# Half of the seven-product FFN's passes with the same weights joined to 512 columns, on one Trainium2 core

## The chip, the cores and the metric

The kernel runs on one core of one Trainium2 chip. Its engines each work through their own queue in order: TensorE (PE) multiplies, VectorE (DVE) and ScalarE (ACT) do the elementwise work, GpSimd (POOL) mainly issues accumulating DMAs, SyncE (SP) issues loads. The metric is the device time of one execution in microseconds.

## The reference

Two decoder layers on 512 tokens of width 1024, in fp32, and a final norm. Each layer has a token mixer, a cross-attention (both with the residual added) and then the gated MLP, on which most of this case turns:

```python
def conv_ffn(x, norm, w_up, dw_w, dw_b, w_down):
    h = rms_norm(x, norm) @ w_up
    g = causal_dwconv(h[..., :D_FF], dw_w, dw_b)
    u = h[..., D_FF:]
    return (jax.nn.gelu(g) * u) @ w_down
```

`D_FF` is 3072, the convolution is 3 tokens wide. The cross-attention's query is `rms_norm(x, norm) @ wq`.

## The kernel before, in words

Activations lie transposed, 128 channels by 512 tokens in a tile (T = 512, M = T/2 = 256, C = 8 tiles of x). An fp32 operand is split into a high part (`high`, a rounding copy by ACT) and a low part (`low`, a subtraction by DVE); a product is three matmuls, high x high, high x low and low x high (`mm3`, lines 186 to 188). A norm keeps its factor r apart: `Norm.feed` multiplies a tile of x by the gain and splits it, the mean of the squares is got by a product with ones into a PSUM bank of its own (`stat`, one buffer; lines 287 and 288), and r is multiplied in later.

The MLP's up-projection makes 24 chunks of 128 gate and 128 value channels. Chunks 0 and 1 are plain products (`start` in `opening`, 24 matmuls of 512 columns each). Each chunk from 2 (`first`) on is a `unit`: a 2 x 2 block product (gate and value by left and right half of the tokens) by seven products in place of eight. A product is four blocks of three matmuls of 256 columns. Chain G adds a11 x B11 and a12 x B21 and gives the gate's left half. Chain F starts as a copy of the first of these (ACT, line 928), then adds s2 x T2, s3 x T3 and a22 x T4; it is read three times, after s2 (into `u`, left), after s3 (into `u`, right) and at the end (the value's left half). Chain H adds s1 x T1 and s4 x B22; with `u` it gives both right halves. The B operands are halves of the norm's tiles, the T operands sums of halves made ahead.

The weights a11, a12, a22, z and r are loaded; s1 to s4 come from them by accumulating DMAs on POOL (lines 825, 828, 830), each issued behind a `low`, and are then split (ACT line 815, DVE line 822). One PSUM pool (`main_ps`) serves G, F and H. The order in a unit, on every engine, is that of the code in `unit`: TensorE has s1, s2, a12, s3, then from unit 4 on the down-projection of an earlier group of four chunks (24 matmuls of 512 columns, tile `aux`), then a11 of the next unit (`ahead`), s4 and a22. `gating` of a unit is a generator whose pieces run in the next unit (`next(left)`): add of H, multiplication by r, the convolution's first tap on ACT (line 895), the other two on DVE (line 898), gelu, the product with f (line 914), and the split of the result (lines 917 and 919), which the down-projections use. The down weights' split is lines 200 (ACT) and 203 (DVE).

At an MLP's opening the plain products cover the mean and r. The tiles of x get their last contribution just before, so the order of `start`'s blocks is made such that the last tile and the mean come late.

## Time and profile before

| | |
|---|---|
| median of three runs | 1432.15 us (1432.05 to 1433.4) |
| profiled execution | 1431.55 us |
| its span | 1429.8 us |
| mean granted TensorE clock | 0.999 |
| TensorE busy | 1417.3 us, 99% of the span |
| VectorE, ScalarE busy | 1074.0 and 900.6 us |

A row of a timeline has the start in us, the duration, engine and line, the operation with what it writes and reads, and in brackets the idle time of its engine ahead of it with what ended that. TensorE's matmuls overlap: one of 256 columns lasts 0.28 us, and the next begins 0.12 us after it. DVE and ACT instructions overlap by about 0.1 us.

### The profile page before, as it was taken

The numbers are of one execution on the slowest core, as the hardware profiler recorded it, in microseconds if no ns is written. First come the engines' busy times: TensorE is split into PE (matmuls) and PEld (weight loads), VectorE is DVE, ScalarE is ACT, GpSimd is POOL, SyncE is SP. The second block draws the span as 40 slices with busy tenths as digits, with TensorE's granted clock in tenths as the row PEclk, the third lists the DMA queues.
The fourth block names the chain that finished last, engine by engine and source line by source line (L and its number), as shares of the span: only waits on it lengthen the run. The fifth ranks groups of instructions, "written<-read, shape, count | busy, mean of one in ns | idle before, by whom it ended". The sixth has DMA issues, their size and how long they took to land.

```text
span 1429.8 us, 22834 instructions
## 1 busy us (share of the span) xinstructions
PE 1417.3 (99%) x8650; PEld 1261.6 (88%) x8650; DVE 1074.0 (75%) x1796; ACT 900.6 (63%) x1592; POOL 316.9 (22%) x333
## 2 busy tenths in 40 slices
PE   9999999999999999999999999999999999999998
PEld 7888888998999999999988777899889999999997
DVE  6987776778776676667798997978787676676665
ACT  7678754667555666666665547667665665666664
POOL 0011310210122222222008992010002222222111
PEclk9999999999999999999999999999999999999999
DMA  8522232544487777777432354345438777777741
GB/s 303 195 75 103 89 124 76 119 110 147 99 199 165 171 172 166 168 171 167 133 133 89 119 162 148 108 87 139 118 86 197 175 177 164 170 175 164 175 120 60
DMA packets 80031, 204.33 MB, mean 143 GB/s; under 512 B 9008, under 2 KB 9520, under 8 KB 79920
## 3 DMA queue, kind: packets, MB, share of 16 engines
q1 hardware_dynamic: 50832, 150.15, 32.8%
q0 software_dynamic: 28800, 52.44, 21.5%
q8 instruction: 68, 1.11, 0.3%
q14 instruction: 43, 0.35, 0.1%
q10 hardware_dynamic: 288, 0.27, 0.1%
HBM read 145.16 MB, written 2.10 MB: 103 GB/s over the span
## 4 chain that ended last, share of the span: by engine, by line
PE 89%; DVE 4%; POOL 2%; ACT 2%; issue 1%; DMA 1%; SPq 0%; POOLq 0%; DVEq 0%; ACTq 0%
PE mm L188 21%; PE mm L186 21%; PE mm L187 21%; PE aux L187 7%; PE aux L186 7%; PE aux L188 7%; PE mm L458 2%; DVE wlo L167 1%; DMA raw<-in_wv 1%; POOL actf L1498 1%; ACT whi L166 1%; PE aux L532 0%; POOL act L167 0%; POOL tmp L1319 0%; DMA raw<-in_wo 0%
## 5 line engine op out<-in xcount | busy, mean ns | idle before, releaser
L186 PE MATMUL mm<-act,whi 128*128 128x512 f32 (+2 forms) x1061 | 368.9, 349 | 0.7 <-ACT act L274 0.6
L187 PE MATMUL mm<-act,whi 128*128 128x512 f32 (+2 forms) x1061 | 369.1, 348 | 0.3 <-DVE act L181 0.2
L188 PE MATMUL mm<-act,wlo 128*128 128x512 f32 (+2 forms) x1061 | 369.0, 348 | 0.0
L186 PEld LDWEIGHTS mm<-act,whi 128*128 128x128 f32 x1061 | 200.5, 189 | 28.3 <-ACT act L274 1.3
L187 PEld LDWEIGHTS mm<-act,whi 128*128 128x128 f32 x1061 | 200.7, 189 | 27.4 <-DVE act L167 1.0
L188 PEld LDWEIGHTS mm<-act,wlo 128*128 128x128 f32 x1061 | 200.7, 189 | 25.1 <-DVE wlo L167 0.6
L822 DVE TENSOR_TENSOR bigr<-raw,bigr 128x512 fp32r<-128x512 f32 x176 | 120.8, 688 | 131.6 <-ACT bigr L815 127.9
L188 PE MATMUL mm<-bigr,bigr 128*128 128x256 f32 x704 | 199.4, 283 | 1.7 <-DVE bigr L822 1.7
L186 PE MATMUL mm<-bigr,bigr 128*128 128x256 f32 x704 | 199.2, 283 | 0.0
L187 PE MATMUL mm<-bigr,bigr 128*128 128x256 f32 x704 | 199.2, 283 | 0.0
L815 ACT ACTIVATE bigr<-raw 128x512 fp32r<-128x512 f32 x176 | 109.0, 621 | 79.1 <-DVE wlo L203 75.9
L828 POOL DMA_DIRECT2D raw<-wa x100 | 87.9, 899 | 309.0 <-DVE bigr L822 215.2
L186 PE MATMUL aux<-act,whi 128*128 128x512 f32 x399 | 155.7, 390 | 0.0
L187 PE MATMUL aux<-act,whi 128*128 128x512 f32 x399 | 155.7, 390 | 0.0
L188 PE MATMUL aux<-act,wlo 128*128 128x512 f32 x399 | 155.2, 389 | 0.0
L166 ACT ACTIVATE whi<-raw 128x1024 fp32r<-128x1024 f32 (+1 forms) x95 | 96.5, 1020 | 87.6 <-PE mm L187 45.2
L188 PEld LDWEIGHTS mm<-bigr,bigr 128*128 128x128 f32 x704 | 135.1, 192 | 2.1 <-DVE bigr L822 2.1
L186 PEld LDWEIGHTS mm<-bigr,bigr 128*128 128x128 f32 x704 | 135.2, 192 | 0.0
L187 PEld LDWEIGHTS mm<-bigr,bigr 128*128 128x128 f32 x704 | 135.2, 192 | 0.0
L825 POOL DMA_DIRECT2D raw<-raw x50 | 43.2, 864 | 366.5 <-DVE wlo L822 347.3
L167 DVE TENSOR_TENSOR wlo<-raw,whi 128x1024 fp32r<-128x1024 f32 (+1 forms) x75 | 90.3, 1210 | 19.5 <-ACT whi L166 19.0
L188 PEld LDWEIGHTS aux<-act,wlo 128*128 128x128 f32 x399 | 74.9, 188 | 15.8
(353 smaller groups left out, 3040.8 us busy)
## 6 DMA issues: line engine op xcount, KB each, us to landing
raw<-wa POOLq DMA_DIRECT2D x150, 256.0 KB, 3.4
wa<-in_wpair SPq DMA_DIRECT2D x88, 256.0 KB, 3.7
raw<-in_wpair SPq DMA_DIRECT2D x44, 512.0 KB, 3.8
big<-in_wdown SPq DMA_DIRECT2D x42, 512.0 KB, 4.4
raw<-raw POOLq DMA_DIRECT2D x50, 256.0 KB, 3.7
raw<-in_pw SPq DMA_DIRECT2D x24, 512.0 KB, 3.3
raw<-in_win SPq DMA_DIRECT2D x20, 512.0 KB, 3.3
raw<-in_wk SPq DMA_DIRECT2D x16, 512.0 KB, 3.3
```

Source lines behind the costliest of these rows:

```text
L166: A.activation(hi, src, AF.Copy)
L167: fetched[1] = (eng or V).tensor_tensor(lo, src, hi.bitcast(F32), op=ALU.subtract)
L186: PE.matmul(ps, wh, xh, start=first, stop=False, skip_group_check=onto)
L187: PE.matmul(ps, wh, xl, start=False, stop=False, skip_group_check=onto)
L188: return PE.matmul(ps, wl, xh, start=False, stop=last, skip_group_check=onto)
L458: PE.matmul(p, m[j], x, start=k == 0 and j == 0 and x is hi, stop=k == C - 1 and x is lo)
L815: A.activation(self.w[name][0], self.block(name), AF.Copy)
L822: V.tensor_tensor(lo, self.block(name), hi.bitcast(F32), op=ALU.subtract)
L825: G.dma_start(self.r, self.z, accum_op=ALU.add)
L828: G.dma_start(block, self.a22, accum_op=ALU.add)
L1498: G.tensor_tensor(z[:, s:], z[:, s:], f[:, s:], op=ALU.add)
```

## The change

The norm's tiles and the T operands are kept as [high | low] of one half of the tokens, 256 + 256 columns, so that the weight's high part meets both in one matmul of 512 columns. For units 4 to 23 (`c > second`) the five products of G and F are, per block, one matmul of 512 columns and one of 256 (the weight's low part by the operand's high). The sum then lies in two halves of a bank, and `gather` adds them when it is read: an ACT copy of the right half and a DVE add of the left. s1 and s4 stay as they were, but H now lies in the `stat` bank. G and F take a full bank each, and F's seed copies 512 columns. For units 4 and 5 one more matmul writes F's bank, ahead of the seed.

r is multiplied into the whole 512 columns of g and of f, from SBUF. Since the norm's tiles lie by halves, `feed` works in two halves, and the plain products (`start`) and the attention's `query` are done in two halves of 256 columns. The opening's order is changed, and in unit 3 the down weights' split is moved behind that of s1 and s2.

```diff
@@ -209 +209 @@
         return hi[:, i : i + n], lo[:, i : i + n]
 
 
+    def parts(x):
+        return x[:, :M], x[:, M:]
+
@@ -218 +221 @@
 
         def feed(self, c):
             g = col(self.gain[0], self.gain[1] + c)
-            hi, lo = act_r(), act_r()
-            A.activation(hi, X[c], AF.Copy, scale=g)
-            self.last = V.scalar_tensor_tensor(lo, X[c], g, hi.bitcast(F32), op0=ALU.mult, op1=ALU.subtract)
-            self.x[c] = (hi, lo)
+            self.x[c] = act_r(), act_r()
+            halves = [(parts(x), X[c][:, i * M : (i + 1) * M]) for i, x in enumerate(self.x[c])]
+            for (hi, _), x in halves:
+                A.activation(hi, x, AF.Copy, scale=g)
+            for (hi, lo), x in halves:
+                self.last = V.scalar_tensor_tensor(lo, x, g, hi.bitcast(F32), op0=ALU.mult, op1=ALU.subtract)
@@ -473 +478 @@
 
         def query(n, w):
             ps = mm_ps()
-            for i, k in enumerate(PAIRED):
-                mm3(ps, blk(w, k * P), norm.x[k], i == 0, i == C - 1)
+            for half in range(2):
+                for i, k in enumerate(PAIRED):
+                    mm3(parts(ps)[half], blk(w, k * P), parts(norm.x[k][half]), i == 0, i == C - 1)
@@ -740 +746 @@
         def fourth(self, k):
-            split(self.t4[:, k * M : (k + 1) * M], *[x[:, M:] for x in self.norm.x[k]])
+            split(self.t4[:, k * M : (k + 1) * M], *parts(self.norm.x[k][1]))
 
@@ -760 +766 @@
             if self.t4 is not None:
                 t4 = self.t4[:, at]
             V.scalar_tensor_tensor(t4, t2, -1.0, b21, op0=ALU.mult, op1=ALU.subtract)
-            for (hi, _), t in zip(self.t, (t1, t2, t3, t4)):
-                A.activation(hi[:, at], t, AF.Copy)
+            both = [self.block(self.T1 + j, k) for j in range(len(self.t))]
+            for x, t in zip(both, (t1, t2, t3, t4)):
+                A.activation(x[:, :M], t, AF.Copy)
             yield
-            for (hi, lo), t in zip(self.t, (t1, t2, t3, t4)):
-                V.tensor_tensor(lo[:, at], t, hi[:, at].bitcast(F32), op=ALU.subtract)
+            for x, t in zip(both, (t1, t2, t3, t4)):
+                V.tensor_tensor(x[:, M:], t, x[:, :M].bitcast(F32), op=ALU.subtract)
+
+        def block(self, j, c):
+
+            if j - self.T1 == len(self.t):
+                return self.norm.x[c][1]
+            if j >= self.T1:
+                return self.t[j - self.T1][c // 2][:, c % 2 * T : (c % 2 + 1) * T]
+            return self.norm.x[c if j == self.B11 else c + 4][j == self.B22]
 
         def product(self, ps, w, j, first=True):
+
             for c in range(4):
-                if j - self.T1 == len(self.t):
-                    x = blk(self.norm.x[c], M, M)
-                elif j >= self.T1:
-                    x = blk(self.t[j - self.T1], c * M, M)
+                (wh, wl), x = blk(w, c * P), self.block(j, c)
+                if ps.shape[-1] == T:
+                    steps = [(ps, wh, x), (ps[:, :M], wl, x[:, :M])]
+                    for i, (to, part, by) in enumerate(steps if c < 3 else steps[::-1]):
+                        PE.matmul(
+                            to, part, by, start=first and c == 0 and i == 0, stop=c == 3 and i == 1, skip_group_check=True
+                        )
                 else:
-                    x = blk(self.norm.x[c if j == self.B11 else c + 4], M if j == self.B22 else 0, M)
-                mm3(ps, blk(w, c * P), x, first and c == 0, c == 3, not first)
+                    mm3(ps, (wh, wl), parts(x), first and c == 0, c == 3, not first)
             return ps
@@ -900 +918 @@
+        def gather(out, ps):
+
+            A.activation(out, ps[:, M:], AF.Copy)
+            add(out, ps[:, :M], out)
+
         def gating(c, g, f, u, F, H):
-            add(g[:, right_half], H, u[:, :M])
-            V.tensor_tensor(g[:, right_half], g[:, right_half], norm.r[:, right_half], op=ALU.mult)
+            if c > second:
+                add(g[:, right_half], H, u[:, :M])
+                V.tensor_tensor(g, g, norm.r, op=ALU.mult)
+            else:
+                add(g[:, right_half], H, u[:, :M])
+                V.tensor_tensor(g[:, right_half], g[:, right_half], norm.r[:, right_half], op=ALU.mult)
             conv = gate_conv(c, g)
             y = next(conv)
             yield
-            times_r(f, F, left_half)
+            if c > second:
+                gather(f[:, left_half], F)
+                V.tensor_tensor(f, f, norm.r, op=ALU.mult)
+            else:
+                times_r(f, F, left_half)
             next(conv)
             yield
             next(conv)
@@ -923 +954 @@
 
         def ahead(c):
 
-            G, F = main_ps()[:, :M], main_ps()[:, :M]
+            G = bank(c)
+            F = bank(c) if c > second else parts(main_ps())[1]
             m(c, G, "a11", seven.B11)
+            if c in (second + 1, second + 2):
+                w = pairs[c].w["a11"]
+                PE.matmul(F, w[0][:, :P], seven.block(seven.B11, 0), start=True, stop=True)
             A.activation(F, G, AF.Copy)
             return G, F
+
+        def bank(c):
+            return main_ps() if c > second else main_ps()[:, :M]
 
         def unit(c):
 
             nonlocal left, chains
             G, F = chains
             down, seeded = downs.get(c), c > GC
-            H = main_ps()[:, :M]
+            H = stat_ps()[:, :M]
             m(c, H, "s1", seven.T1)
             if c <= second:
                 high(c + 1, "s3")
@@ -943 +981 @@
 
             m(c, F, "s2", seven.T2, False)
             u, f, g = tmp_f(), tmp_f(), tmp_f()
-            A.activation(u[:, :M], F, AF.Copy)
+            if c > second:
+                gather(u[:, :M], F)
+            else:
+                A.activation(u[:, :M], F, AF.Copy)
             if c == first:
                 both(c + 2, "a11")
             if down:
@@ -961 +1002 @@
                 high(c + 2, "a11")
             low(c, "s4")
             if c > second:
-                times_r(g, G, left_half)
+                gather(g[:, left_half], G)
 
             m(c, F, "s3", seven.T3, False)
-            A.activation(u[:, M:], F, AF.Copy)
+            if c > second:
+                gather(u[:, M:], F)
+            else:
+                A.activation(u[:, M:], F, AF.Copy)
             add(f[:, right_half], H, u[:, M:])
             if c <= second:
                 times_r(g, G, left_half)
             if c == second:
                 low(c + 2, "a11")
             low(c + 1, "a22")
-            V.tensor_tensor(f[:, right_half], f[:, right_half], norm.r[:, right_half], op=ALU.mult)
+            if c <= second:
+                V.tensor_tensor(f[:, right_half], f[:, right_half], norm.r[:, right_half], op=ALU.mult)
             both(c + 2, "a11")
             high(c + 1, "a12")
             low(c + 1, "a12")
@@ -983 +1028 @@
                 pairs[c + 3].load()
             if c + 2 in pairs and c > first:
                 pairs[c + 2].load_second()
-            if c >= GC - 1 and c + 1 in downs:
+            if c > second and c + 1 in downs:
                 downs[c + 1].w.high()
                 downs[c + 1].w.low()
             if c + 2 in downs and first < c <= CF - 2:
@@ -992 +1037 @@
             low(c + 1, "s1")
             high(c + 1, "s2")
             low(c + 1, "s2")
+            if c == second:
+                downs[c + 1].w.high()
+                downs[c + 1].w.low()
             if down:
                 down.home(0, d[0], seeded)
 
@@ -1010 +1058 @@
             nonlocal left, chains
             ps, y = {}, {}
 
-            def start(i, ks=range(C)):
-                if ks[0] == 0:
+            def start(i, half, ks=range(C)):
+                if half == 0 and ks[0] == 0:
                     ps[i] = main_ps()
                 for k in ks:
-                    mm3(ps[i], blk(w[i], k * P), norm.x[k], k == 0, k == C - 1)
+                    mm3(parts(ps[i])[half], blk(w[i], k * P), parts(norm.x[k][half]), k == 0, k == C - 1)
 
@@ -1036 +1084 @@
             ss = split(norm.ss)
-            start(0, range(C - 1))
-            start(1, range(2))
-            start(0, (C - 1,))
+            start(0, 0, range(C - 1))
+            start(1, 0, range(C - 1))
+            start(0, 0, (C - 1,))
             fetch(2)
             w[-1].low()
             mean = mean_of(ss)
@@ -1048 +1096 @@
...
             V.reciprocal(norm.r, root)
-            start(1, range(2, C))
+            start(1, 0, (C - 1,))
+            start(0, 1)
+            start(1, 1)
@@ -1062 +1112 @@
-            start(2)
+            start(2, 0)
+            start(2, 1)
@@ -1074 +1125 @@
-            start(3)
+            start(3, 0)
+            start(3, 1)
             chains = ahead(first)
```

DVE's queue between units 3 and 4 of layer 0, before (`bigr` are the low parts of the s weights; row 2 is the low of a12, rows 4 and 5 those of s1 and s2, all of unit 4; L203 is the down weights' low; `mm_3892` is H of unit 3):

```order
L974 TENSOR_TENSOR tmp_3926<-tmp_3926,r_3611 128x256
L822 TENSOR_TENSOR wlo_3802<-wa_3651,whi_3801 128x512
L203 TENSOR_TENSOR wlo_3983<-big_3653,whi_3982 128x1024
L822 TENSOR_TENSOR bigr_3988<-raw_3647,bigr_3988 128x512
L822 TENSOR_TENSOR bigr_3991<-raw_3647,bigr_3991 128x512
L171 TENSOR_TENSOR tmp_3927<-mm_3892,tmp_3925 128x256
L905 TENSOR_TENSOR tmp_3927<-tmp_3927,r_3611 128x256
```

The same place in the change (line 840 is the old 822; `stat_4068` is H of unit 3, and the same bank takes s1 of unit 4):

```order
L1019 TENSOR_TENSOR tmp_4102<-tmp_4102,r_3706 128x256
L840 TENSOR_TENSOR wlo_3978<-wa_3779,whi_3977 128x512
L840 TENSOR_TENSOR bigr_4160<-raw_3775,bigr_4160 128x512
L840 TENSOR_TENSOR bigr_4163<-raw_3775,bigr_4163 128x512
L203 TENSOR_TENSOR wlo_4168<-big_3781,whi_4167 128x1024
L171 TENSOR_TENSOR tmp_4103<-stat_4068,tmp_4101 128x256
L932 TENSOR_TENSOR tmp_4103<-tmp_4103,r_3706 128x256
```

The lows of s1 and s2 now stand ahead of the down weights' low, and the add of H stays right behind all three.

DVE's queue where unit 4 gives way to unit 5, in the change (L929 and L938 are r, L916 the two taps, `mm_4172` is F of unit 4, `mm_4332` F of unit 5):

```order
L171 TENSOR_TENSOR tmp_4237<-stat_4211,tmp_4235 128x256
L929 TENSOR_TENSOR tmp_4237<-tmp_4237,r_3706 128x512
L171 TENSOR_TENSOR tmp_4236<-mm_4172,tmp_4236 128x256
L938 TENSOR_TENSOR tmp_4236<-tmp_4236,r_3706 128x512
L916 SCALAR_TENSOR_TENSOR tmp_4366<-tmp_4237,par,tmp_4366 128x511
L916 SCALAR_TENSOR_TENSOR tmp_4366<-tmp_4237,par,tmp_4366 128x510
L171 TENSOR_TENSOR tmp_4394<-mm_4332,tmp_4394 128x256
```

The add on F after s2 (last row) is a DVE row that was not there, as one ACT copy read F at this point; and the value's left half is gathered and multiplied ahead of the taps.

TensorE's queue at the mean of layer 1's opening, in the change (L292 and L293 are the mean; the 27 rows of 512 columns and the three of tile 7 that led to it are now 42 and three of 256):

```order
L186 MATMUL mm_10899<-act_10871,whi_10885 128x256
L187 MATMUL mm_10899<-act_10871,whi_10885 128x256
L188 MATMUL mm_10899<-act_10871,wlo_10886 128x256
L292 MATMUL stat_10952<-act_10895,ones 128x512
L293 MATMUL stat_10952<-act_10896,ones 128x512
L186 MATMUL mm_10921<-act_10871,whi_10889 128x256
```

Tile 7 of the second piece and all of the right halves now stand behind the mean.

## The prediction

> **What bounds the kernel now.** I read the page first (busy time by engine, then the chain that ended last), then the waits of TensorE, then timelines at the places that the change touches.
>
> ```profile
> span 1429.8 us, 22834 instructions
> PE 1417.3 (99%) x8650; PEld 1261.6 (88%) x8650; DVE 1074.0 (75%) x1796; ACT 900.6 (63%) x1592; POOL 316.9 (22%) x333
> PE 89%; DVE 4%; POOL 2%; ACT 2%; issue 1%; DMA 1%; SPq 0%; POOLq 0%; DVEq 0%; ACTq 0%
> ```
>
> TensorE is the bound: 99% busy and 89% of the chain that ended last. So the time moves in two ways only: TensorE's own work gets shorter, or TensorE waits. The waits of TensorE name the two that this change can touch:
>
> ```profile
> PE mm L188 <- DVE bigr L822: 1.7, 2, 0.8
> ...
> PE stat L288 <- DVE act L167: 0.2, 1, 0.2
> ```
>
> The first is in each layer where unit 4 starts; the second is the column sums' mean at an FFN opening. All else that the diff edits is covered today, which means that it may uncover itself.
>
> **TensorE's own work.** What a matmul costs is its distance to the next one, since they overlap. The windows view gives it for 24 down matmuls of 512 columns (its count of 26 takes in two that reach over the edges) and for 72 of 256; the timeline has 512 columns again, 27 from its first row to its second.
>
> ```profile
> 561.11:566.58 5.47, 5.47 (x26) 4.51 (x25) 4.77 (x10) 4.24 (x8) 0.86 (x1) 1.00 0.64 172
> 566.58:575.21 8.63, 8.63 (x73) 8.62 (x72) 5.55 (x9) 3.96 (x8) 2.58 (x3) 1.00 0.80 163
> ```
>
> ```profile
> 1041.87 0.39 PE L186 MATMUL mm<-act,whi 128*128 128x512 f32 x1
> ...
> 1047.99 0.39 PE L186 MATMUL mm<-act,whi 128*128 128x512 f32 x1
> ```
>
> 5.47/24 = 0.228 and 6.12/27 = 0.2267 us for 512 columns, 8.63/72 = 0.1199 for 256. A 512-column pass is therefore cheaper than two of 256 (0.2398) by 12 to 13 ns.
>
> - Merged: 20 units in each of 2 layers, 5 products, 4 blocks: 800 times three matmuls of 256 (360 ns) become one of 512 and one of 256 (347 to 348 ns). 800 x 12.2 to 13.3 ns = 9.8 to 10.6 us less.
> - Split: `query` and the four `start`s, 2 + 4 pieces in each of 2 layers, 24 matmuls each: 288 of 512 columns become 576 of 256. 288 x 12.2 to 13.3 ns = 3.5 to 3.8 us more.
> - Four extra 512 matmuls in `ahead`: 4 x 0.227 = 0.9 us more.
>
> TensorE's work falls by 5.4 to 5.9 us; I take **5.5**. [...]
>
> **Unit 3 to unit 4, both layers.** Here H moves into the column sums' only bank, and the down weights' high and low are moved behind those of s1 and s2. Today, in layer 0:
>
> ```profile
> 392.00 0.86 POOL L828 DMA_DIRECT2D raw<-wa  x1 [2.07 <-DVE bigr L822]
> ...
> 395.80 1.05 ACT L200 ACTIVATE whi<-big 128x1024 fp32r<-128x1024 f32 x1
> ...
> 398.23 1.22 DVE L203 TENSOR_TENSOR wlo<-big,whi 128x1024 fp32r<-128x1024 f32 x1
> 399.11 0.63 ACT L815 ACTIVATE bigr<-raw 128x512 fp32r<-128x512 f32 x1 [1.75 <-PE mm L188]
> 399.36 1.29 DVE L822 TENSOR_TENSOR bigr<-raw,bigr 128x512 fp32r<-128x512 f32 x2
> 400.10 0.38 PE L188 MATMUL mm<-bigr,bigr 128*128 128x256 f32 x1 [0.83 <-DVE bigr L822]
> ```
>
> ```profile
> DMA to landing us min/median/max: 3.7/4.3/7.0
> ```
>
> TensorE waits at 400.10 for the low part of s1, which stands behind the down weights' low (398.23). The edit puts s1 ahead of it, so this wait goes. But s1 of unit 4 now writes the bank in which H of unit 3 lies, and so waits for DVE's add of H, and in DVE's queue that add stands behind the down weights' low. Its high (1.05 on ACT) stands behind the high of s2, which waits for the accumulating DMA issued at 392.00: 7.0 us, the longest of three in that stretch (the second fence, the source view of line 828), so 399.0, just before ACT's 399.11. From there (an instruction begins about 0.1 before the one ahead ends: 398.23 to 399.36 is 1.13 for a duration of 1.22): ACT high of s2 0.54, down high 1.05, DVE low 1.14 and the add 0.42, with 0.1 for the handovers: 399.11 + 3.25 = 402.36 for s1's first matmul. Without any wait its first two matmuls would stand 0.24 ahead of the 400.10 that is there, at 399.86. So 2.5 us more is the upper end. If the DMA lands earlier, DVE's own queue is the lower one: from 398.23 two lows (0.60 each), the down low (1.14), the add (0.42): 401.0, 1.2 us more. I take 1.8, twice: **+3.6**. Nothing pays it back behind, as TensorE has no other work in its queue ahead of s1.
>
> **FFN opening.** The mean comes after 45 matmuls of 256 (5.4 us) in place of 30 of 512 (6.8 us).
>
> ```profile
> 1048.52 0.69 DVE L167 TENSOR_TENSOR act<-tmp,act 128x512 fp32r<-128x512 f32 x1 [0.76 <-ACT act L166]
> 1048.67 0.39 PE L287 MATMUL stat<-act,ones 128*128 128x512 f32 x1
> 1049.26 0.50 PE L288 MATMUL stat<-act,ones 128*128 128x512 f32 x1 [0.20 <-DVE act L167]
> ```
>
> In layer 1 TensorE reached the mean at 1048.67 and already waited for the low sums (1048.52 + 0.69). 1.4 us earlier it waits that much longer; the sums come no sooner, as the last feed, now two halves, costs DVE and ACT a bit more. I take 1.25. Layer 0 has no such wait in the waits view, so its cost lies between nothing and layer 1's; I take 0.25, nearer to nothing, as the sums there are ready before TensorE comes. Together **+1.5** (1.25 to 2.5). `query` needs its last x 2.2 us sooner by the same order; by rows of that place it just meets it, **+0.1**.
>
> **Layer end.** TensorE's last down products wait for the last unit's gating, and that chain gets longer.
>
> ```profile
> 1396.14 0.42 DVE L171 TENSOR_TENSOR tmp<-mm,tmp 128x256 f32<-128x256 f32 x1
> ...
> 1397.05 0.82 ACT L895 ACTIVATE tmp<-tmp,par 128x512 f32<-128x512 f32 x1 [1.60 <-DVE tmp L905]
> 1397.90 1.54 DVE L898 SCALAR_TENSOR_TENSOR tmp<-tmp,par,tmp 128x511 f32<-128x511 f32 x2 [0.55 <-ACT tmp L895]
> ...
> 1400.97 0.62 ACT L917 ACTIVATE act<-tmp 128x512 fp32r<-128x512 f32 x1
> 1401.33 0.94 PE L186 MATMUL mm<-act,whi 128*128 128x384 f32 x3
> 1401.62 0.69 DVE L919 TENSOR_TENSOR act<-tmp,act 128x512 fp32r<-128x512 f32 x1 [0.73 <-ACT act L917]
> ```
>
> TensorE's three matmuls at 1401.33 took 0.94 instead of 0.68, so it is just waiting here for the high at 1400.97. After: add of H 0.46; r over 512 columns 0.73 (0.69 as at 1401.62, and a handover) in place of 0.46; ACT's first tap 0.72 (0.82 less the overlap); F's right half copied behind it 0.42 (0.38, as the 573.97 row below has it, and a handover); DVE's add of it 0.46; r over 512 columns 0.61; and only then the two taps. They start at 1396.14 + 3.40 = 1399.54 in place of 1397.90, 1.6 us later, and the high with them. Layer 0:
>
> ```profile
> 712.32 1.06 ACT L166 ACTIVATE whi<-raw 128x1024 fp32r<-128x1024 f32 x1 [1.57 <-DMA raw<-in_wdown]
> ...
> 713.41 1.23 DVE L167 TENSOR_TENSOR wlo<-raw,whi 128x1024 fp32r<-128x1024 f32 x1 [0.29 <-ACT whi L166]
> 714.56 0.68 DVE L914 SCALAR_TENSOR_TENSOR tmp<-tmp,tmp 128x512 f32<-128x512 f32 x1
> 715.28 0.63 ACT L917 ACTIVATE act<-tmp 128x512 fp32r<-128x512 f32 x1 [1.37 <-DVE tmp L914]
> ```
>
> The second tap, late by the same, falls behind the low at 713.41, which a DMA holds: a tap and ACT's gelu, 0.75 + 0.67, come between it and 714.56, 1.4 more. Together **+3.0** (1.5 if the H add comes earlier than today).
>
> **The loop of units.** Nothing waits there today.
>
> ```profile
> 573.97 0.38 ACT L946 ACTIVATE tmp<-mm 128x256 f32<-128x256 f32 x1 [2.58 <-PE mm L188]
> ...
> 576.46 0.69 DVE L822 TENSOR_TENSOR bigr<-raw,bigr 128x512 fp32r<-128x512 f32 x1 [3.50 <-ACT bigr L815]
> ```
>
> The s3 product may write F again once s2's sum is read. Today one ACT copy at 573.97 does that; now it is a copy and a DVE add, and the add stands in DVE's queue behind the whole front of the gating: from the end of s4, 0.20 to the H add, then the 3.40 of the layer end, two taps 1.44, the add 0.42 and a handover 0.05, together 5.51 us. TensorE has a22, s1, s2 and a12 in between: s1 12 x 0.12 = 1.44, the three merged ones 4 x 0.347 = 1.39 each, 5.60. When DVE is the later of the two at the H add, as in this loop by 0.1, the slack is about nil: 0 to 0.15 us a unit, 38 units, 0 to 5.7. It is nearer to the lower end, as DVE's 3.50 us of idle time soaks up any lag after it; I take 0.03 a unit, **+1.2**.
>
> **Sum.** -5.5 + 3.6 + 1.5 + 0.1 + 3.0 + 1.2 = +3.9. The profiled execution took 1431.55 us (span 1429.8); the median of the runs is 0.6 above it. 1431.55 + 3.9 = **1435.5 us**.
>
> **Rivals.**
> - *The waits stay covered* (0.2): the work of TensorE falls by 5.5 and the waits cost at most half of 8.2. For it: each wait is worked out from queue order, and an earlier DMA or add takes it away; against it: the chain at unit 4 holds even with an early DMA. 1431.55 - 5.5 = 1426 to 1430.
> - *The loop decides* (0.2): s3 waits in every unit. The lag of DVE at H's add is 0.1 or more and carries over; then 0.15 x 38 = 5.7 in place of 1.2, 1440. From 0.15 a unit the merges (5 x 4 x 13 ns = 0.26 a unit) lose more than half to it. Against it: the 3.50 us of idle time on DVE.
> - *No gain from the merge* (0.05): in the 256-column stretch above the weight loads are busy for 8.62 of 8.63 us, in the 512-column stretch for 4.51 of 5.47; if passes of both widths in turn ran no faster than today's three, the splits and the waits would stand alone: 1431.55 + 3.7 + 0.9 + 9.4 = 1445. Against it: a pass in turn loads no more weights than before, and 512 columns leave more time for each load.
> - My forecast, the gain paid back at the seams (0.55): 1432 to 1438.
>
> What a measurement of this kernel can tell from no change is 0.2%, 2.9 us: below 1429.3 is faster, above 1435.0 slower. The forecast lies at the edge of it, and its part is split nearly evenly. Slower: 0.25 + 0.2 + 0.05 less a little, 0.48. Same: 0.30 + 0.05 from the first rival, 0.35. Faster: 0.17. The range reaches from half-covered waits to the loop's full price: 1427.5 to 1441; the likeliest case by itself, 1432 to 1438.
>
> **What would show it.** The merged F product should take 4 x 0.347 = 1.39 us, a unit 15.29 in place of 15.55. Right at unit 4: TensorE waits for the H add (before, for a low of L822), 1 to 3 us, twice. At the mean in layer 1: a wait of 1 us or more. At a layer's end: the last high 1.4 us later relative to the down products. In the loop: a TensorE wait for DVE's add ahead of s3, or none. I am wrong if TensorE has no wait of 1 us at unit 4, or if a unit takes 15.4 or more.

## The result: slower by 0.85%, outside the range

| | before | after |
|---|---|---|
| median | 1432.1 us (1430.93 to 1433.4, 6 executions) | 1444.38 us (1442.98 to 1447.02, 6 executions) |
| ratio | | 1.0085, interval 1.0075 to 1.0096 |
| profiled execution, its span | 1431.55, 1429.8 us | 1442.98, 1441.2 us |
| mean granted TensorE clock | 0.999 | 0.995 |

Executions disturbed by far more than any effect here (1735, 1998, 2349 and 3688 us) are left out of every median.

The forecast was 1435.5 us, 1427.5 to 1441. The direction is right (+3.9 was forecast, the profiled execution shows +11.4), the size is not. The page of the changed kernel, against the three lines with which the prediction begins:

```profile
span 1441.2 us, 22110 instructions
PE 1421.0 (99%) x8142; PEld 1239.8 (86%) x8142; DVE 1131.2 (78%) x1908; ACT 939.2 (65%) x1704; POOL 317.1 (22%) x333
PE 88%; DVE 4%; ACT 2%; POOL 2%; DMA 2%; issue 2%; SPq 0%; POOLq 0%; ACTq 0%; DVEq 0%
```

TensorE has 508 matmuls fewer and yet is busy 3.7 us longer. The share of 99% hides both: waits are there, and busy time is not always time at the full clock. TensorE's waits in the changed kernel (what waits, for what, then total us, how often, the longest):

```profile
PE stat L186 <- DVE tmp L171: 6.9, 2, 3.8
PE mm L186 <- ACT act L279: 1.5, 1, 1.5
...
PE stat L293 <- DVE act L167: 0.4, 2, 0.2
```

The first row is s1 of unit 4 waiting for DVE's add of H, as forecast. It is 6.9 us in place of the 1.7 of the old wait at that point.

**Unit 3 to unit 4.** The timeline of layer 0, to be laid beside the rows at 392.00 to 400.10 in the prediction:

```profile
394.80 0.86 POOL L846 DMA_DIRECT2D raw<-wa  x1 [2.07 <-DVE bigr L840]
...
401.63 0.63 ACT L833 ACTIVATE bigr<-raw 128x512 fp32r<-128x512 f32 x1 [2.40 <-DMA raw<-wa]
402.16 1.04 ACT L200 ACTIVATE whi<-big 128x1024 fp32r<-128x1024 f32 x1
402.29 0.69 DVE L840 TENSOR_TENSOR bigr<-raw,bigr 128x512 fp32r<-128x512 f32 x1 [0.58 <-ACT bigr L833]
403.24 1.23 DVE L203 TENSOR_TENSOR wlo<-big,whi 128x1024 fp32r<-128x1024 f32 x1 [0.25 <-ACT whi L200]
404.38 0.42 DVE L171 TENSOR_TENSOR tmp<-stat,tmp 128x256 f32<-128x256 f32 x1
404.94 0.39 PE L186 MATMUL stat<-bigr,bigr 128*128 128x256 f32 x1 [3.01 <-DVE tmp L171]
405.14 0.41 PE L187 MATMUL stat<-bigr,bigr 128*128 128x256 f32 x1
...
407.26 0.41 PE L188 MATMUL stat<-bigr,bigr 128*128 128x256 f32 x1
```

This is the forecast chain link by link: accumulating DMA, high of s2, high of the down weights, their low, the add, s1. From ACT's 401.63 it takes 3.31 us to s1 at 404.94, where 3.25 was worked out. The DMA is where the time is: issued at 394.80, it let ACT go at 401.63, 6.8 us later. The bracket counts from the modelled end of the matmul before; by the distance of the two matmuls the wait is 3.17 us, and waits are given by that distance below where no row stands beside them. The last two rows show something else: from the second to the last of s1's twelve matmuls it is 2.12 us for ten distances, 0.212 us each, in place of 0.12.

The windows view shows why. Its columns are the stretch, its length, the busy time of PE, PEld, DVE, ACT and POOL with counts, then the granted clock, the DMA share and GB/s:

```profile
401.71:405.12 3.41, 0.40 (x3) 0.23 (x3) 2.54 (x5) 1.98 (x3) 1.07 (x2) 1.00 0.90 215
405.12:408.53 3.41, 3.41 (x15) 3.23 (x15) 1.97 (x4) 0.81 (x1) 0.65 (x1) 0.50 0.87 168
408.53:411.95 3.42, 3.42 (x22) 3.01 (x21) 1.36 (x3) 1.95 (x4) 0.00 (x0) 1.00 0.51 175
...
1098.03:1101.44 3.41, 1.93 (x9) 1.96 (x10) 2.83 (x5) 1.04 (x2) 1.54 (x2) 0.50 0.82 168
1101.44:1104.85 3.41, 3.41 (x14) 3.02 (x14) 0.77 (x2) 0.00 (x0) 0.00 (x0) 0.50 0.47 112
```

The edges are put where the granted clock changes, and one such window further out. It is 0.50 for 3.41 us in layer 0 and for 6.83 us in layer 1, where s1 begins at 1099.51, inside the first of the two windows; then it is back. TensorE counts as busy from s1 on. What this costs shows against the wide-tile kernel below, whose clock stays full at this place: from s1's first matmul to unit 4's first down product, 36 matmuls, it takes 5.73 us in both layers, and the changed kernel takes 7.23 and 8.13. The half clock costs 1.5 and 2.4 us.

**Between the layers.** DVE's timeline at the end of layer 0's MLP, before:

```profile
731.38 1.27 DVE L866 TENSOR_TENSOR x<-x,mm 128x512 f32<-128x512 f32 x2
732.64 1.23 DVE L167 TENSOR_TENSOR wlo<-raw,whi 128x1024 fp32r<-128x1024 f32 x1
```

The two adds into x come first, then the low of a mixer weight. The same two in the changed kernel:

```profile
736.37 1.23 DVE L167 TENSOR_TENSOR wlo<-raw,whi 128x1024 fp32r<-128x1024 f32 x1 [0.31 <-ACT whi L166]
737.51 1.28 DVE L884 TENSOR_TENSOR x<-x,mm 128x512 f32<-128x512 f32 x2
```

The low now stands ahead of the adds (and waits for ACT). Layer 1's first norm needs these adds, so its column sums come later, and TensorE has used up most of its other products by then. The windows view of that stretch:

```profile
741.75:746.14 4.39, 1.83 (x10) 0.99 (x9) 3.47 (x9) 1.12 (x4) 0.00 (x0) 1.00 0.00 0
746.14:749.80 3.66, 3.48 (x9) 2.66 (x10) 3.66 (x6) 2.26 (x4) 0.00 (x0) 0.54 0.00 0
```

TensorE is busy 1.83 of 4.39 us there, and then runs 3.66 us at a clock of 0.54. This place is no part of the diff and no step of the prediction spoke of it.

**The units.** ACT's first tap of the convolution comes once a unit. Two of them that are 16 units apart in layer 0, in the kernel before:

```profile
430.71 0.82 ACT L895 ACTIVATE tmp<-tmp,par 128x512 f32<-128x512 f32 x1 [0.48 <-DVE tmp L905]
679.35 0.81 ACT L895 ACTIVATE tmp<-tmp,par 128x512 f32<-128x512 f32 x1 [0.48 <-DVE tmp L905]
```

And in the changed one:

```profile
437.48 0.82 ACT L913 ACTIVATE tmp<-tmp,par 128x512 f32<-128x512 f32 x1 [0.33 <-DVE tmp L929]
683.16 0.82 ACT L913 ACTIVATE tmp<-tmp,par 128x512 f32<-128x512 f32 x1 [0.33 <-DVE tmp L929]
```

248.64/16 = 15.54 us a unit before, 245.68/16 = 15.355 after. The merge gives 0.185 us a unit, 40 x 0.185 = 7.4 us in all, and nothing waits in the loop.

The ledger, from the distances between TensorE's matmuls at these places (after less before, us):

| place | forecast | measured |
|---|---|---|
| merged products, with what the loop gives back | -9.8 to -10.6 and +1.2 | -7.4 |
| `query` and `start` in halves | +3.5 to +3.8 | +3.8 |
| extra matmuls of 512 (two of the four are counted with the units) | +0.9 | +0.5 |
| wait for `query`'s last x | +0.1 | 0 |
| mean at the openings | +1.5 | +1.3 |
| wait at unit 4, both layers | +3.6 | +5.2 |
| half clock behind that wait | 0 | +3.9 |
| layers' ends | +3.0 | +0.1 |
| seam to layer 1's mixer | 0 | +3.1 |
| attention of layer 1 (differs between executions) | 0 | +0.3 |
| assigned to no place | 0 | +0.6 |
| sum | +3.9 | +11.4 |

### The profile page after: what moved, and what is told of

It is laid out like the page before. It is cut to its first block, busy times and chain, and to the rows that moved or that the text cites. A ratio compares the mean times of both kernels' runs of the same rounds, so it can differ in the third digit from the quotient of the medians.

```text
span 1441.2 us, 22110 instructions
## 1 busy us (share of the span) xinstructions
PE 1421.0 (99%) x8142; PEld 1239.8 (86%) x8142; DVE 1131.2 (78%) x1908; ACT 939.2 (65%) x1704; POOL 317.1 (22%) x333
## 3 DMA queue, kind: packets, MB, share of 16 engines
q8 instruction: 64, 1.05, 0.3%
## 4 chain that ended last, share of the span: by engine, by line
PE 88%; DVE 4%; ACT 2%; POOL 2%; DMA 2%; issue 2%; SPq 0%; POOLq 0%; ACTq 0%; DVEq 0%
PE mm L791 19%; PE mm L187 12%; PE mm L186 12%; PE mm L188 12%; PE aux L186 7%; PE aux L187 7%; PE aux L188 7%; PE stat L186 3%; PE stat L188 3%; PE stat L187 3%; PE mm L463 2%; DMA raw<-wa 1%; DMA raw<-in_wv 1%; POOL actf L1550 1%; PE aux L538 0%
## 5 line engine op out<-in xcount | busy, mean ns | idle before, releaser
L186 PE MATMUL mm<-act,whi 128*128 128x512 f32 (+2 forms) x837 | 295.2, 354 | 1.7 <-ACT act L279 1.5
L187 PE MATMUL mm<-act,whi 128*128 128x512 f32 (+2 forms) x837 | 296.3, 354 | 0.3 <-DVE act L181 0.2
L188 PE MATMUL mm<-act,wlo 128*128 128x512 f32 (+2 forms) x837 | 295.8, 353 | 0.0
L791 PE MATMUL mm<-bigr,bigr 128*128 128x512 f32 x960 | 190.0, 341 | 0.0
L186 PEld LDWEIGHTS mm<-act,whi 128*128 128x128 f32 x837 | 158.1, 189 | 24.2 <-ACT act L279 2.0
L187 PEld LDWEIGHTS mm<-act,whi 128*128 128x128 f32 x837 | 158.5, 189 | 22.9 <-DVE act L167 1.0
L188 PEld LDWEIGHTS mm<-act,wlo 128*128 128x128 f32 x837 | 158.5, 189 | 21.0 <-DVE wlo L167 0.6
L791 PEld LDWEIGHTS mm<-bigr,bigr 128*128 128x128 f32 x960 | 149.2, 190 | 18.3
L171 DVE TENSOR_TENSOR tmp<-mm,tmp 128x256 f32<-128x256 f32 x202 | 80.7, 418 | 51.7 <-ACT tmp L923 50.4
L791 PE MATMUL mm<-act,whi 128*128 128x512 f32 x320 | 119.4, 396 | 0.0
L923 ACT ACTIVATE tmp<-mm 128x256 f32<-128x256 f32 x160 | 55.5, 372 | 81.4 <-PE mm L791 81.4
L187 PEld LDWEIGHTS aux<-act,whi 128*128 128x128 f32 x399 | 74.9, 188 | 15.9
```

The source lines that it names most:

```text
L171: V.tensor_tensor(out, a, b, op=ALU.add)
L186: PE.matmul(ps, wh, xh, start=first, stop=False, skip_group_check=onto)
L187: PE.matmul(ps, wh, xl, start=False, stop=False, skip_group_check=onto)
L188: return PE.matmul(ps, wl, xh, start=False, stop=last, skip_group_check=onto)
L791: PE.matmul(to, part, by, start=first and c == 0 and i == 0, stop=c == 3 and i == 1, skip_group_check=True)
L923: A.activation(out, ps[:, M:], AF.Copy)
```

## Experiments

Two theories stood after the result. **The bank**: the time is lost because s1 of unit 4 waits for H, so a wait, and the clock that falls behind it, are the cause. **The layout**: the halves, the extra adds on DVE and the merged passes themselves cost it, and the waits would move elsewhere. All ratios are against the kernel before, run beside the kernel on the same chip.

**H back in the main pool.**

```diff
-            H = stat_ps()[:, :M]
+            H = main_ps()[:, :M]
```

> The change, with chain H back in the pool of G and F instead of the column sums' bank. Theory (the loss is the wait of unit 4's s1 for the add of H, 3.17 and 4.01 us in the two layers, and the lower clock right behind each wait): no such wait, no lower clock in the two stretches behind it, 11 to 12 us less than the change, 1431 to 1433 us. Rival (the clock falls for another reason, such as the denser work of the merged passes): the waits go, 7 us less, and the clock still falls near 400 and 1100 us. Second rival (the bank is not it; the adds of two halves make the loop slow): 1443 us as the change.

Measured: 1438.66 us, 1.0046 (1.0031 to 1.0061): 6.7 us over the kernel before in place of 12.3. TensorE's timeline at units 4 and 5, one row of layer 0 and two of layer 1:

```profile
404.91 1.68 PE L791 MATMUL mm<-bigr,bigr 128*128 128x512 f32 x8 [0.76 <-ACT mm L963]
...
1097.65 1.69 PE L791 MATMUL mm<-bigr,bigr 128*128 128x512 f32 x8 [1.90 <-ACT mm L963]
1101.97 1.68 PE L791 MATMUL mm<-bigr,bigr 128*128 128x512 f32 x8 [1.23 <-DVE tmp L171]
```

The wait for H and both stretches of half clock at unit 4 are gone, 5.2 + 3.9 = 9.1 us by the ledger, yet the time is not the 1431 to 1433 us that was expected. But s2 now waits for the copy that seeds F (ACT line 963, which stands behind the high of the down weights), and s3 for DVE's add of u: 5.5 us of new waits in the two rows of the waits view (2.8 and 2.7). More than half of what the bank cost comes back at the same place. Both theories get a part: the bank is a cause, and behind it lies the next one.

**The down weights' split ahead again, as before.**

```diff
-            if c > second and c + 1 in downs:
+            if c >= GC - 1 and c + 1 in downs:
...
-            if c == second:
-                downs[c + 1].w.high()
-                downs[c + 1].w.low()
```

> The change, with H in the column sums' bank, but the down weights' split of unit 3 put back ahead of s1 and s2. The H add is then behind s2's low only. Theory: the wait of unit 4's s1 falls by ACT's 1.05 and DVE's 1.14 us, to about 1.3 in layer 0 and 2.1 in layer 1, and so short a wait leaves the clock at full: 3.7 us from the waits and 4 from the clock, 1435 to 1437 us. Rival (the clock falls after any wait above that of the kernel before, 0.99 us): 3.7 us less alone, 1439 to 1440.

Measured: 1442.01 us, 1.0066 (1.0051 to 1.0081), the waits 2.14 and 3.67 us. The order of the split is 1.4 us of the two waits (7.2 in the change), where 3.7 were expected; the rest stays. What tells more is the clock. TensorE's row behind the first wait, and then the windows behind both:

```profile
403.72 0.36 PE L186 MATMUL stat<-bigr,bigr 128*128 128x256 f32 x1 [1.98 <-DVE tmp L171]
```

```profile
403.72:407.60 3.88, 3.88 (x17) 3.62 (x18) 2.15 (x4) 0.81 (x1) 1.54 (x2) 0.58 0.86 170
1098.69:1104.00 5.31, 5.31 (x21) 4.92 (x22) 2.15 (x4) 0.81 (x1) 1.56 (x2) 0.50 0.79 158
```

The clock fell behind both waits, behind the short one too.

**The add of H ahead of s2's and the down weights' split in unit 3.**

```diff
-            high(c + 1, "s2")
-            low(c + 1, "s2")
-            if c == second:
-                downs[c + 1].w.high()
-                downs[c + 1].w.low()
+            if c != second:
+                high(c + 1, "s2")
+                low(c + 1, "s2")
...
             next(left)
+            if c == second:
+                high(c + 1, "s2")
+                low(c + 1, "s2")
+                downs[c + 1].w.high()
+                downs[c + 1].w.low()
```

> The change, with H in the column sums' bank, but in unit 3 the splits of s2 and of the down weights moved behind the first piece of the gating, so that DVE adds H as soon as s4 is done. Theory (it is the place of the add in DVE's queue, not the bank): the wait at unit 4 is under 0.5 us, the clock stays full there, 1431.5 to 1434 us. Rival (the bank itself makes the wait, as TensorE needs it at once): at least 0.9 us a layer from s4's end to the add's, and s2 late by its split, 1435 or more.

Measured: 1438.1 us, 1.004 (1.0026 to 1.0054): 6.2 us over the kernel before. TensorE's rows in layer 1:

```profile
1094.80 0.36 PE L186 MATMUL stat<-bigr,bigr 128*128 128x256 f32 x1 [0.27 <-DVE tmp L171]
1097.26 1.44 PE L791 MATMUL mm<-bigr,bigr 128*128 128x256 f32 x7 [0.22 <-DVE bigr L840]
1100.86 1.68 PE L791 MATMUL mm<-bigr,bigr 128*128 128x512 f32 x8 [0.75 <-DVE tmp L171]
```

With H still in the `stat` bank its wait is down to 0.27 us, and the clock stays full there. So it is the place of the add in DVE's queue, not the bank as such, that made the wait long. The waits for s2's low and for the add of u remain, some 2 us a layer, and in this profile the seam between the layers has half clock for two windows (743.29 to 750.12); the 1431.5 to 1434 us that were expected did not come.

**The adds into x at the layer's end by priority.**

```diff
-                    downs[CF + j].sum(i, ps)
+                    with tc.high_priority(URGENT):
+                        downs[CF + j].sum(i, ps)
```

> The change, with only the adds of the last down-projections to x given priority on DVE, at the end of layer 0's MLP. Theory (of the 3.1 us lost between the layers the cause is the order of DVE's queue there: the last two adds stand behind a weight's low that waits for a transfer, so the token norm is late): the waits of TensorE near 743 to 747 fall from 3.3 us to about 1 and the clock stays full there, 2.5 to 3.5 us less, 1440 to 1441.5. Rival (the seam is late by the gating of the last unit, as forecast): no change there, 1443 to 1444.5.

Measured: 1442.77 us, 1.0075 (1.0058 to 1.0092), not to be told from the change by its time. From the end of layer 0's last unit to the end of the seam this kernel loses 1.5 us against before, where the change loses 3.3, and the clock stays full, as the windows view shows:

```profile
742.50:747.50 5.00, 2.72 (x19) 2.16 (x17) 4.24 (x7) 1.94 (x3) 0.00 (x0) 1.00 0.64 227
747.50:751.00 3.50, 3.19 (x19) 2.67 (x20) 3.46 (x7) 2.07 (x5) 0.00 (x0) 1.00 0.03 12
```

TensorE's wait for ACT's line 279 at the seam, 1.8 us by the distance where the kernel before has 0.8, is as in the change, so the order of the two adds is not all of the loss. And the waits at unit 4 were longer in that profile (its waits view), and took the gain back:

```profile
PE stat L186 <- DVE tmp L171: 7.8, 2, 4.2
```

The order there is the same as in the change, where it was 6.9, and half clock lasted two windows in layer 0 in place of one (8.43 us to the first down product in place of 7.23). So these waits differ between executions, and with the clock by as much as the seam is worth.

**The joined passes taken apart again, all else as in the change.**

```diff
-                    steps = [(ps, wh, x), (ps[:, :M], wl, x[:, :M])]
+                    steps = [(ps[:, :M], wh, x[:, :M]), (ps[:, M:], wh, x[:, M:]), (ps[:, :M], wl, x[:, :M])]
```

> The change with each joined pass of 512 columns done as two of 256 into the same two halves of the bank; layout, adds, banks and order as in the change. It prices the merge alone. Theory (a joined pass saves 12 to 13 ns, and 800 of them 9.8 to 10.6 us, of which a lag of the loop takes some back): a unit 15.54 to 15.60 us in place of 15.355, 1451 to 1455 us. Rival (in turn with 256 columns a joined pass saves less, about 10 ns, and nothing waits in the loop): 7.5 to 8 us more, a unit 15.55, 1450 to 1452 us.

Measured: 1450.82 us, 1.0128 (1.0111 to 1.0145). The same two first taps as above:

```profile
438.17 0.82 ACT L913 ACTIVATE tmp<-tmp,par 128x512 f32<-128x512 f32 x1 [0.35 <-DVE tmp L929]
686.81 0.81 ACT L913 ACTIVATE tmp<-tmp,par 128x512 f32<-128x512 f32 x1 [0.35 <-DVE tmp L929]
```

248.64/16 = 15.54 us a unit, that of the kernel before. So the joined passes by themselves give 0.185 us a unit; the extra adds and copies of the loop cost TensorE nothing. This speaks against the layout theory in its main part, and prices the merge below the 12 to 13 ns a pass of the theory, as the rival had it: 6.3 us in the medians (18.6 over the kernel before in place of 12.3), 7.4 by the units.

**The kernel before with H in the `stat` bank and the down weights' split moved.** No halves, no joined passes.

```diff
-            H = main_ps()[:, :M]
+            H = stat_ps()[:, :M]
...
-            if c >= GC - 1 and c + 1 in downs:
+            if c > second and c + 1 in downs:
...
+            if c == second:
+                downs[c + 1].w.high()
+                downs[c + 1].w.low()
```

> The kernel before with two edits alone: H in the column sums' bank, and the down weights' split of unit 3 behind those of s1 and s2. Theory (these two make the wait of 3 to 4 us at unit 4 and the lower clock behind it): 2.2 and 3 us of wait net of today's 0.99, and 2 to 2.7 of clock in each layer, 1440 to 1443 us, with no loss anywhere else. Rival (the wait takes the merged passes and the adds of halves): under 1436 us.

Measured: 1440.78 us (1435.31 to 1442.25), 1.0056 (1.0034 to 1.0077). TensorE's row behind the wait in layer 0, and the windows with the wait and behind it:

```profile
400.79 0.36 PE L186 MATMUL stat<-bigr,bigr 128*128 128x256 f32 x1 [2.11 <-DVE tmp L171]
```

```profile
397.88:401.29 3.41, 1.30 (x11) 1.13 (x11) 3.38 (x7) 1.41 (x4) 0.95 (x2) 1.00 0.88 232
401.29:404.71 3.42, 3.42 (x18) 3.42 (x18) 1.65 (x3) 0.67 (x1) 0.86 (x1) 0.50 0.51 95
```

Two edits out of the whole change, put on the old kernel, make it 8.6 us slower. This is the strongest evidence for the bank: the wait and the half clock are there without one joined pass. The profiled execution is 10.6 us over that of before: 0.3 us ahead of it up to layer 0's unit 4, then 5.4 behind by the two units 4. The rest comes between the two, although no edit lies there: 0.3 at the seam, 3.0 at the column sums of layer 1's mixer (TensorE waits there 2.21 us in place of 0.78, and a window of half clock follows), and 2.2 in the attention and the opening behind it. The spread of the four times (1435.31 to 1442.25) says that not every execution has all of it.

**Three cures on the change**: the add of H ahead, the adds into x by priority, and the mean later.

```diff
             start(0, 0, (C - 1,))
+            start(1, 0, (C - 1,))
+            start(0, 1, range(3))
```

> The change with three edits: in unit 3 the splits of s2 and the down weights behind the first piece of the gating, the mean two passes of tile 7 and nine matmuls later, and priority on DVE for the last adds to x. Theory (the three places are independent, and each gives back what its stretch lost): 5.7 us as measured for the first, 1.3 for the mean, 2.1 for the seam, 1434 to 1436 us, no lower clock anywhere ahead of the last 40 us. Rival (a place relieved gives its wait to the next): 1437 to 1439.

Measured: 1434.8 us, 1.002 (1.001 to 1.0029), clock 0.999, as expected. The mean's wait is gone, the waits at unit 4 are as in the kernel with the add of H ahead. Of the 12.3 us that the change loses, 2.6 are left, by moving work in queues alone.

**The same, with u's left half copied whole by ACT and added from SBUF**, so that F is free after one copy.

```diff
-                gather(u[:, :M], F)
+                A.activation(u, F, AF.Copy)
+                add(u[:, :M], u[:, :M], u[:, M:])
```

> The three edits, and the sum after s2 read by ACT whole, both halves at once, with the add of the halves then from SBUF: F is free for s3 after ACT alone. Theory (s3 of units 4 and 5 waits 0.9 and 0.35 us for DVE's add, as it stands behind the gating): these waits go, 2 to 2.6 us less than with the three edits, 1431.5 to 1434 us. Rival (ACT, 0.2 us longer in every unit, is late elsewhere): no change or slower.

Measured: 1432.5 us, 1.0008 (0.9998 to 1.0018). That the add of u no longer holds s3 is not shown by a profile of this kernel; the wide tile with the same edit ("Wide tile and cures together", below) has no row of s3 against DVE's add in its waits view. By its time the change is now level with the kernel before, and not under it; the splits of `query` and `start` alone (3.8 us) take half of what the merge gives.

**A wide norm tile instead of halves.** Each tile of the norm is one of 1024 columns, high and low side by side; a joined pass reads two runs of 256 from it. `query`, `start`, `feed` and the opening's order are as before.

```diff
+                    out = ps if len(x.shape) == 2 else ps.rearrange("p (a b) -> p a b", a=2)
...
+            both = self.norm.both[k].rearrange("p (a b) -> p a b", a=2)[:, :, at : at + M]
```

> The change, with high and low of a norm's tile in one tile of 1024 columns, so that the joined pass reads the two halves as two runs 512 columns apart; the query and the plain products go back to 512 columns, and the opening to its old order. It prices the splits and the earlier mean. Theory: 288 splits at 13.3 ns, 3.84 us, and the mean's 1.3 less than the change, the waits at unit 4 as they are, 1438 to 1441 us, a unit 15.35 us. Rival (two runs in one pass read slower, or the high part's readers wait for the low's write): a unit over 15.40, 1443 or more.

Measured: 1436.53 us, 1.0035 (1.0021 to 1.0048), 4.2 us over the kernel before in place of 12.3: the splits and the wait for the mean are gone, and a unit takes 15.36 us, so a joined pass over two runs costs what one over 512 adjoining columns costs. The waits for H are still there. TensorE's rows behind them, and then the windows around the first, cut at whole multiples of 3.41 us from the half clock that this profile has at the seam, from 745.3 on (see the last section):

```profile
402.26 0.36 PE L199 MATMUL stat<-bigr,bigr 128*128 128x256 f32 x1 [2.52 <-DVE tmp L184]
...
1094.80 0.36 PE L199 MATMUL stat<-bigr,bigr 128*128 128x256 f32 x1 [2.83 <-DVE tmp L184]
```

```profile
400.56:403.97 3.41, 1.71 (x13) 1.73 (x14) 2.83 (x5) 1.26 (x2) 0.86 (x1) 1.00 0.98 213
403.97:407.39 3.42, 3.42 (x21) 2.98 (x20) 1.97 (x4) 1.95 (x4) 0.86 (x1) 1.00 0.59 80
```

Yet the clock behind the first is 1.00, though this wait is longer than those of 1.98 and 2.11 us above that were followed by half clock; behind the second it is 1.00 too. So the length of a wait alone does not part these cases. By the multiples an edge lies at 400.56: it cuts the first wait in two, and no window holds more than 1.7 us of it. So part of the gain is luck: the 1438 to 1441 us of the theory counted the half clock of unit 4, and this profile happens to have none.

**Wide tile and cures together**: the add of H ahead, the adds into x by priority, u copied whole.

> The wide layout together with the gating ahead of the splits in unit 3, the last adds to x first on DVE, and the sum after s2 read whole by ACT: all of the change's gain with none of the costs that were found. Theory: 3.84 less than the three edits with the whole read (1433.5), 1428 to 1431 us, under the kernel before. Rival (a place relieved gives its wait to the next): 1432 or more.

Measured: 1434.72 us, 1.0016 (1.0008 to 1.0025), so the rival holds (counted from the 1432.5 us above, the theory's 3.84 less would be 1428.7). TensorE is through with layer 0's MLP (its first key product of the seam) 1.9 us ahead of the kernel before, and at the column sums of layer 1's mixer it is 3.4 us behind it (1.64 and 1.77 us of waits at the seam and half clock behind them). What TensorE gained in the units it waits for there.

**The same with H in the main pool.**

> The wide layout and its three edits, with chain H back in the pool of G and F, so that neither unit 4 nor unit 5 waits for the add of H. Theory: the waits for it there, 0.42, 0.23 and 0.88 us in each layer, go, 2.5 to 3 us less than with H in the column sums' bank (1434.7), 1431.5 to 1432.5. Rival (s2 or s3 of unit 4 takes the wait over, as with H back and nothing else): 1433.5 or more.

Measured: 1433.71 us, 1.0007 (0.9998 to 1.0016). With u copied whole and the splits late, the main pool serves H again without the wait of the first experiment. Over the kernel before it is 1.1 us in place of 2.4, but the intervals overlap, and s2 now waits for its high (two waits, 1.1 us in all), as the rival has it.

**Two of the mixer's weight splits of layer 1 behind its norm's diagonals**, on the last one.

```diff
+                with tc.issue_after(drawn[0]):
+                    weights()
+                    fetch()
+                    weights()
+                    fetch()
```

> The same, and between the layers two of the next mixer's weights are split only behind the token norm's diagonals, so that DVE does not hold these behind a weight's low that waits for a transfer. Theory (3 us are lost there in the wide layout, 1.6 and 1.8 us of waits and a lower clock behind them): no wait over 1 us there but the 0.9 that the kernel before has, 1428 to 1430.5 us, under the kernel before. Rival (the waits come from the squares' sum itself): as the run beside it.

Measured: 1431.93 us, 0.9997 (0.9988 to 1.0006). The seam's waits are 2.23 and 1.51 us in this profile, and half clock lies behind them: the splits are not the only thing that holds it.

**Twelve key matmuls of the seam behind the norm's first spreading product**, on the last one, so that TensorE has work while DVE does the norm.

```diff
-            key2 = mem.products(parked[2], ks=range(4))
+            with tc.issue_after(spreads[0]):
+                key2 = mem.products(parked[2], ks=range(4))
```

> The wide layout with H in the pool of G and F, its three edits and the late weights, and between the layers 12 matmuls of a key product kept behind the first of the token norm's spreading products, so that TensorE has work while DVE and ACT make the first scaled tile. Theory (the seam costs by order alone: TensorE's filling work stands ahead of the chain in place of beside it): the waits of 2.2 and 1.5 us there fall to 1.5 in all, no lower clock there, 3 us less than the run without (1431.9), 1428 to 1430 us. Rival (the wait moves ahead of the spreading products, with the same sum): 1431 to 1433.

Measured: 1430.77 us, 0.9985 (0.9976 to 0.9994). No half clock at the seam, though 0.83, 1.47 and 1.51 us of waits are left, where 1.5 in all were expected: there are three shorter waits with products between them. Whether the edit or the place of the windows kept the clock full, one profile does not tell.

**The last one with s2's split back in its place**, only the down weights' split behind the add of H.

```diff
+            high(c + 1, "s2")
+            low(c + 1, "s2")
...
             if c == second:
-                high(c + 1, "s2")
-                low(c + 1, "s2")
                 downs[c + 1].w.high()
                 downs[c + 1].w.low()
```

> The same, but in unit 3 only the down weights' split stands behind the gating, and the split of s2 is back ahead of it. With H out of the column sums' bank nothing of s1 waits, and s2's high is no longer behind the gating's first tap. Theory: unit 4's waits of 0.7 and 0.5 us in each layer go, 2 us less than the run beside it, 1426 to 1428.5 us. Rival (the waits of unit 4 pass on to s3, as it did with H back and nothing else): the same as the run beside it.

Measured: 1430.35 us, 0.9985 (0.9976 to 0.9994), faster than both kernels, if only by 2.1 us of 1432.42, and not to be told from the run before it (1430.77). The first rows of its waits view:

```profile
PE mm L199 <- ACT act L292: 1.4, 1, 1.4
PE mm L200 <- DVE act L194: 1.2, 1, 1.2
PE stat L152 <- POOL onesf L141: 1.0, 1, 1.0
```

Nothing of unit 4 is in these first rows; the first two are the seam, which has a window of half clock again. A unit takes 15.33 us. TensorE is through with layer 0's MLP 4.0 us ahead of the kernel before, and at the column sums of layer 1's mixer it is 0.9 us behind it. So the seam, not the units, is where the rest of the gain stays, and no run here cured it whole.

## Why the prediction was wrong

The likeliest case, the gain paid back at the seams, named the right mechanism at unit 4 and missed the time by its size. Step by step:

- **"The merged F product should take 4 x 0.347 = 1.39 us, a unit 15.29": mis-sized.** By its own bound ("I am wrong ... if a unit takes 15.4 or more") 15.355 passes, but 0.26 a unit was counted on and 0.185 came. The prices were taken from stretches of one width (whose rows give 11.8 to 13.0 ns a merge, a little less than the 12.2 to 13.3 that were written); in turn a pair costs a little more. TensorE's rows of one merged product in unit 3, four pairs from the first row to the second:

```profile
397.26 0.40 PE L791 MATMUL mm<-act,whi 128*128 128x512 f32 x1
...
398.67 0.40 PE L962 MATMUL mm<-act,whi 128*128 128x512 f32 x1
```

  1.41/4 = 0.3525 us a pair (the median in the loop is 0.351) against 0.347 forecast and 0.360 for three of 256 columns. In the units 0.185/20 = 9 ns a merge, not 12 to 13: 7.4 us in place of 9.8 to 10.6. The rival that saw no gain from the merge falls with it.
- **The loop, "+1.2": not there.** The wait, put at 0 to 0.15 us a unit, is nothing: in the unit at 570 us DVE's add ends at 579.74 and s3 begins at 579.90. The distance of the units is even, and the waits view has no row of s3 against DVE. The rival in which the loop decides falls. Where the slack is smaller, at units 4 and 5, the mechanism is real: with H in the main pool s3 waits 1.4 us there for just that add.
- **Splits, "3.5 to 3.8": right**, 3.8.
- **FFN opening, "+1.5": right as a sum by luck, wrong in its parts.** Both layers wait alike, about 0.9 us each (before: none and 0.47), so 0.9 and 0.4 more, where 0.25 and 1.25 more were forecast. The last link of layer 1's wait in the changed kernel:

```profile
1055.75 0.50 PE L293 MATMUL stat<-act,ones 128*128 128x512 f32 x1 [0.23 <-DVE act L167]
```

  The old wait there was 0.20 (1049.26). Layer 0 was taken "nearer to nothing" since no wait stood in the view; no wait in a view says only that the slack is above zero, not that it is 1.4 us.
- **Unit 3 to unit 4, "+3.6": the mechanism right, the size short, 5.2.** The chain from ACT's start to s1 came out at 3.31 against 3.25. What failed is "I take 1.8": the value was put between a bound in which the DMA lands as before (2.5) and one in which it lands early (1.2). Layer 0 came to 2.2, near the first, layer 1 to 3.0, over it. The slow landing that the view showed once in three was treated as bad luck and was the rule in both layers (6.7 and 7.6 us, source view of line 846 in the changed kernel).
- **The step that failed outright: "TensorE's work" was priced at one clock.** The prediction costed each wait at its own length. Behind the waits of 3.2 and 4.0 us the clock stood at half for 3.41 and 6.83 us, 3.9 us more, three quarters of what the waits cost. Of the 7.5 us by which the sum is short, this is the largest part; the seam adds 3.1 (with a window of half clock of its own), the wait at unit 4 and the merge 1.6 each, and the layers' ends give 2.9 back. The kernel before has a granted clock of 0.999 and no wait over 1.0 us at unit 4, so the profile of before shows no such price; the clock was read there and taken to be fixed.
- **Layer end, "+3.0": the chain was right and the cover was wrong.** The timeline of the changed kernel at the end of layer 1, the add of H on DVE and the last high on ACT:

```profile
1407.34 0.42 DVE L171 TENSOR_TENSOR tmp<-stat,tmp 128x256 f32<-128x256 f32 x1
...
1413.73 0.63 ACT L948 ACTIVATE act<-tmp 128x512 fp32r<-128x512 f32 x1 [0.76 <-DVE tmp L945]
```

  6.39 us, against 4.83 before (1396.14 to 1400.97): 1.56 longer, with 1.6 forecast. But TensorE waits 0.2 us only, as its queue now has more down products ahead of this high than it had (15 behind the four transposes of line 1188, in place of 7). The order of those rows could have been counted beforehand, as that at unit 4 was.
- **The seam between the layers: not seen.** 3.1 us. The scheduler put a weight's low ahead of two adds that the next norm needs. The diff does not touch that place; only a look at the whole order of DVE there would have shown it. Giving the adds priority took the loss from 3.3 to 1.5 us, layer's end included, so their order is a cause of about half of it; what makes the rest was not found. The same place costs 4 to 5 us in kernels with other edits and 0.3 in the old kernel with two, so it shifts with edits that do not touch it.

The rival in which the waits stay covered falls with the first row of the waits view. The range reached to 1441 for a loop that waits in every unit, and left out that a wait may cost half its length or more again in clock.

## What to carry to other kernels

When TensorE is the bound and a change makes it wait in one place, count the wait and then, as a risk, a window or two of half clock behind it: at unit 4 it came behind waits of 1.98 to 4.17 us by the brackets, though not behind 2.52 and 2.83 with the wide tile, and cost 1.5 and 2.4 us in the change. Here a bank that changed hands put the queue of the engine that frees it onto the critical path (waits of 3.17 and 4.01 us, and 0.27 in layer 1 with the freeing read ahead): look at what stands ahead of the freeing read, and put that read first. And compare the order of the two kernels at places that the diff does not touch, above all where a scheduler fills in between stages.

## What the hardware showed

- **Half clock came behind stretches of 3.41 us in which TensorE was busy for little of the time.** In the change the granted clock is 1.00 or 0.50, and up to the last products it changes only at points that lie whole multiples of 3.41 us apart (405.12, 408.53, 746.45, 749.86, 1098.03, 1104.85). In other executions the points lie elsewhere: 401.29 and 404.71 in the old kernel with two edits, 743.29 and 750.12 with the add of H ahead. A window is a stretch of 3.41 us between such points or their multiples. At unit 4, a window at full clock in which TensorE was busy 1.43 us or less was followed by half clock: 0.40 and 1.05 us in the change, 1.43 and 1.36 with the down weights ahead, 1.30 and 1.31 in the old kernel with two edits, 0.55 and 0.82 with the adds into x by priority, 0.24 and 0.17 with the passes apart. One in which it was busy 1.71 us or more was not: 1.71, 1.91 and 2.08 with the wide tile, 2.17 or more with H in the main pool. At the seam, where matmuls stand singly, busy time does not part the cases at the same place: windows busy for 1.32 us in the change, but also for 1.81 with the wide tile and 1.82 with the add of H ahead, were followed by half clock.
- **The length of a wait alone did not part the cases.** Waits of 1.98 and 2.11 us (by the brackets) that fell into one window were followed by half clock, and those of 2.52 and 2.83 that an edge cut in two were not. That the place of the wait decides is the author's reading of these rows; no run here sets it by itself. At unit 4 half clock lasted one window, and a second one where TensorE still waited in the first (busy 1.93 of 3.41 us in layer 1 of the change).
- **Passes of 512 and 256 columns in turn cost 0.351 us a pair** (median of the loop), some 4 ns more than 0.2267 and 0.1199 in stretches of their own; a 512-column pass whose operand lies in two runs of 256 costs no more than one in a single run (15.36 us a unit in both).
- **The wait behind one accumulating DMA differs between layers and executions of the same order**: 3.17 and 4.01 us in the change, 3.78 and 4.33 with the adds into x by priority.
